# Strassen's seven block products for pairs of FFN input column blocks, with weight sums made by adding DMA transfers

## The chip, the cores and the metric
One core of one Trainium2 chip. The metric is device time in microseconds of one execution of the whole program; several executions are timed and their median is taken. The engines are TensorE (PE, with its weight loads listed apart as PEld), VectorE (DVE), ScalarE (ACT), GpSimd (POOL) and SyncE (SP), which here only issues DMA transfers; 16 DMA engines move the data.

## The reference
A decoder trunk of two layers on 256 tokens of width 1024, in float32. Each layer is FFN, mixer, FFN, each followed by a LayerNorm; the mixer is a recurrent block in layer 0 and dilated attention in layer 1. So there are four FFNs (numbered 0 to 3 below), and they hold most of the arithmetic:
```python
def swiglu(x, w_in, w_out):            # w_in 1024 x 5632, w_out 2816 x 1024
    gate, up = jnp.split(x @ w_in, 2, axis=-1)
    return (jax.nn.silu(gate) * up) @ w_out
...
x = layer_norm(DEEPNORM_ALPHA * x + 0.5 * swiglu(x, ...), g, b)
```

## The kernel before
**Precision.** Weights and activations are split into a high part (rounded to fp32r) and a low part (the rest), and each product of 128x128 by 128xN is three matmuls, hi*hi, hi*lo and lo*hi (`mm3`, L90, all recorded as L88).

**Weights.** All weights come from HBM in halves of 128 x 1024 floats (512 KB). `half_piece` (L117) makes one half ready: SP loads it into a `raw` buffer (L126; 4 of them), ACT casts raw to `w_hi` (L127), DVE subtracts to get `w_lo` (L128). There are 10 buffers of `w_hi` and `w_lo` (`WBUFS`). `order_ffn` and its like write the order of all halves into the list `feed`; `pump` emits the next half, `take` hands out the next piece of two halves and pumps what is missing. A cast needs a free weight buffer, so it waits until PE has done with the half ten places earlier; a load needs a free raw buffer, so SP waits for the subtraction four halves earlier. Outside the blocks marked `pinned` the framework's list scheduler orders each engine's queue; each queue then runs strictly in order.

**An FFN** (`ffn`, L337) runs over 11 column blocks j of 256 gate and 256 up columns. In block j, `natural` (L309) multiplies for both token halves t the x of 128 tokens (transposed and split in `xT`) with the block's two w_in pieces: 8 row blocks times 3 matmuls of 512 columns into one PSUM bank, so 48 matmuls. `gate` (L345) makes silu(gate) * up * 0.5 (ACT L347, DVE L350); its `rest` (L352) turns the result on PE (L98) and splits it into `h_hi` and `h_lo` (L104, L105), put off by `flush` to the next block. Then `prj.part` multiplies h of block j-2 with its w_out piece: 24 matmuls of 512 columns into four more banks (`yy`). The last three w_out pieces form the tail, in `Project.finish` (L279), together with LayerNorm (`Norm`, L229; its power, L245, is POOL's only work after the start) and the turning of the new x into `xT`.

**Order of the work.** FFN 0, the recurrent stage, FFN 1, keys and values, FFN 2, attention, FFN 3. The recurrent stage follows a list of steps written out by hand, `RG` (L463), in which `pv` is one pumped half, letters are steps (u, y, g, o on PE; h, b, q, z, e on ACT; and so on); inside `pinned` the engines keep that order. In FFN 0 the late loads (`late_loads`, L196: x for the LayerNorm, parameters, a distance table) and `softplus_prep` stand inside block 4, behind its `natural` (L415).

Of the kernel before, what the change touches and what calls it, by code (L numbers as in the profile page):

```python
# [9 lines left out]
F32 = mybir.dt.float32  # L10
F32R = mybir.dt.float32r
AF = mybir.ActivationFunctionType
ALU = mybir.AluOpType
# [20 lines left out]
PIECE = 2048  # L34
HALF = PIECE // 2
TAIL = 3
WBUFS = 10
KVBUFS = 12
WARM = 17
PRE = 2  # L40
HBUFS = 6
DILATIONS = ((128, 1), (512, 4), (2048, 16))
SLOPES = [float(2.0 ** (-8.0 * (i + 1.0) / HEADS)) for i in range(HEADS)]
# [3 lines left out]
def trunk_kernel(  # L47
# [36 lines left out]
    def two_banks():  # L84
        return psum.tile([P, 1024], F32, name="yy", bufs=2)

    def mm(ps, lhsT, rhs, start, stop):
        tc.keep_in_program_order(nc.tensor.matmul(ps, lhsT=lhsT, rhs=rhs, start=start, stop=stop))  # L88

    def mm3(ps, a, b, first, last):  # L90

        (ahi, alo), (bhi, blo) = a, b
        mm(ps, ahi, bhi, first, False)
        mm(ps, ahi, blo, False, False)
        mm(ps, alo, bhi, False, last)

    def turn(ps, src):
        tc.keep_in_program_order(nc.tensor.transpose(ps, src, ident))  # L98
# [8 lines left out]
    def duo(tag, bufs, pool=act, shape=(2, SEQ)):  # L107
        hi = pool.tile([P, *shape], F32R, name=f"{tag}_hi", bufs=bufs)
        lo = pool.tile([P, *shape], F32R, name=f"{tag}_lo", bufs=bufs)
        return hi, lo  # L110
# [6 lines left out]
    def half_piece(src, low=nc.vector, cuts=1, high=nc.scalar):  # L117
        if low is None:
            w = wts.tile([P, HALF], F32, name="w_full", tag="w_hi", bufs=WBUFS)
            nc.sync.dma_start(w, src)  # L120
            return w
        raw = wts.tile([P, HALF], F32, name="raw", bufs=4)
        w = duo("w", WBUFS, wts, (HALF,))
        for n in range(cuts):
            c = slice(n * HALF // cuts, (n + 1) * HALF // cuts)
            nc.sync.dma_start(raw[:, c], src[:, c])  # L126
            (nc.scalar.copy if high is nc.scalar else high.tensor_copy)(w[0][:, c], raw[:, c])  # L127
            i = low.tensor_tensor(out=w[1][:, c], in0=raw[:, c], in1=f32(w[0][:, c]), op=ALU.subtract)  # L128
        if low in barrier:
            tc.add_manual_dep(i.ins, barrier[low].ins.name, NO_SYNC, reason="after the LayerNorm")  # L130
        return w
# [7 lines left out]
    def pump(n=1, low=None, high=nc.scalar):  # L139

        for _ in range(min(n, len(feed))):
            src, e, cuts = feed.pop(0)
            ready.append(half_piece(src, e and (low or e), cuts, high))

    def take(n=2):

        pump(n - len(ready))
        w, ready[:n] = ready[:n], []
        return w
# [46 lines left out]
    def late_loads():  # L196
        for dst_, src in ((xn[0], x[tok(0), :]), (xn[1], x[tok(1), :]), (par, rg_par), (dst, dist), (qsc, q_scale)):
            tc.keep_in_program_order(nc.sync.dma_start(dst_, src))
# [20 lines left out]
    def load_ln(i, tag="o", bufs=4):  # L219
        gb = [[act.tile([P, 512], F32, name="gb", tag=f"{tag}_{('hi', 'lo')[j]}", bufs=bufs) for j in range(2)]  # L220
              for _ in range(2)]
        for r in range(2):
            for h in range(2):
                tc.keep_in_program_order(
                    nc.sync.dma_start(gb[r][h], ln[i, r, h * 512:(h + 1) * 512].partition_broadcast(P)))
        return gb
# [91 lines left out]
    def channels(ps, w):  # L318

        for m in range(2):  # L320
            channel_half(ps[:, m * SEQ:(m + 1) * SEQ], w, m)

    def order_ffn(idx):
        if not idx:
            for n in range(8):
                h = n // 2 % 2
                order(w_in[idx, 2 * (n % 2) + n // 4], cuts=1 if n else 2, only=slice(h, h + 1))
        for j in range(NJ):
            for q in range(2):
                if idx or j > 1:  # L330
                    order(w_in[idx, 2 * j + q])
            if 0 <= j - 2 < NJ - TAIL:
                order(w_out[idx, j - 2])
        for i in range(NJ - TAIL, NJ):
            order(w_out[idx, i])

    def ffn(ln_i, turn_x, ahead):  # L337
        hs, gated = {}, {}
        later = []

        def flush(keep=0):
            while len(later) > keep:
                later.pop(0)()

        def gate(ps, t, j):  # L345
            sg = work.tile([P, 256], F32, name="sg")
            nc.scalar.activation(sg, ps[:, :256], AF.Silu)  # L347
            if t == 0:
                gated[j] = work.tile([P, NT, 256], F32, name="gated", tag="sc")
            nc.vector.scalar_tensor_tensor(gated[j][:, t, :], ps[:, 256:], 0.5, sg, ALU.mult, ALU.mult)  # L350

            def rest():  # L352
                hh = gated.pop(j)
                pt = bank()
                for m in range(2):
                    for t_ in range(NT):
                        turn(pt[:, (m * NT + t_) * P:(m * NT + t_ + 1) * P], hh[:, t_, m * P:(m + 1) * P])
                split(*hs[j], halves(pt))
            if t:
                later.append(rest)  # L360

        prj = Project(lambda t, k: at(hs[k // 2], k % 2, tok(t)), KF)
        for j in range(2):
            hs[j] = duo("h", HBUFS)
        if turn_x:
            gb = load_ln(ln_i)
            w = [take() for _ in range(3)]
            opened = []
            for t in range(NT):
                ps = bank()  # L370
                natural(ps, t, w[:2])
                flush()
                gate(ps, t, 0)
                if t == 0:
                    turn_x(0)
                ps = bank()
                natural(ps, t, w[2:], range(4))
                opened.append(ps)
                if t == 0:
                    turn_x(1)  # L380
            w3 = take()
            for t in range(NT):
                natural(opened[t], t, (None, w3), range(4, 8))
                flush()
                gate(opened[t], t, 1)
        else:
            with pinned():
                ps = [[bank() for _ in range(NT)] for _ in range(2)]
                for q in range(4):
                    if q:  # L390
                        load_xT(2 * q, 2 * q + 1)
                    else:
                        load_xT(0)
                    for j in range(2):
                        w = take(1)
                        if q == j == 0:
                            load_xT(1)
                        for t in range(NT):
                            natural(ps[j][t], t, {q // 2: {q % 2: w[0]}}, range(2 * q, 2 * q + 2))
                pump(PRE)  # L400
                for j in range(2):
                    for t in range(NT):
                        gate(ps[j][t], t, j)
                    if j == 0:
                        pump(4 - PRE)
        for j in range(2, NJ):
            hs[j] = duo("h", HBUFS)
            w = [take() for _ in range(2)]
            for t in range(NT):
                ps = bank()  # L410
                natural(ps, t, w)
                flush(1 - t if j == 2 else 0)
                gate(ps, t, j)
            if j == 4 and not turn_x:
                late_loads()  # L415
                gb = load_ln(ln_i)
                softplus_prep()
            if 0 <= j - 2 < NJ - TAIL:
                w = take()
                for t in range(NT):  # L420
                    prj.part(t, j - 2, w)
        for i in range(NJ - 2, NJ - TAIL):
            w = take()
            for t in range(NT):
                prj.part(t, i, w)
        tail = [(i, take()) for i in range(NJ - TAIL, NJ)]
        first, second = prj.tail(tail)
        first[2:5] = first[3], first[2], first[4]
        return prj.finish([first, second], gb, (ahead,), flush)
# [15 lines left out]
    def natural_pair(turn_x, then):  # L445
# [3 lines left out]
        for t, ps in enumerate(natural_both(turn_x)):  # L449
# [3 lines left out]
            def rest(t=t, tmp=tmp):  # L453
# [6 lines left out]

    ENGINES = {"v": (nc.vector, nc.scalar), "g": (nc.gpsimd, nc.scalar),
               "V": (nc.vector, nc.vector), "G": (nc.gpsimd, nc.vector)}
    RG = """r0 pv u3 pv pv pv r1 c1 c0 pv pv u2 pv pv u4 pv pv pv pv pv g0 c4 h0 pv pv g1 c2 h1 y0 g2 pv e0 pv y1  # L463
        c3 h2 pv b0 b2 g3 pv g4 pv h3 pv y3 a2 h4 pv b3 pv b4 b1 q01 y2 q34 a01 a34 e1 z1 e3 m01 e2 z0 s0 m4
        s1 F0 F1 z2 y4 pv e4 m3 k0 z4 o0 s4 q2 k1 m2 s2 F2 z3 s3 o1 k2 F4 o2 pv F3 pv k4 k3 T21101""".split()

    def order_recurrent():
        both = (nc.vector, nc.vector)
# [348 lines left out]
        order(o_w[i])  # L817
    order_ffn(3)

    turn_x = ffn(0, None, 4)  # L820
    with pinned():
        turn_x = recurrent(1, turn_x)
    turn_x = ffn(2, turn_x, 4)
    kv = keys_values(turn_x)
    pump(6)
    turn_x = ffn(3, lambda h: None, 4)
    with pinned():
        turn_x = attention(kv, 4, turn_x)
    ffn(5, turn_x, 0)


# [74 lines left out]
```

## Time and profile before
| | |
|---|---|
| median of 3 runs | 1055.94 us (1055.44 to 1056.11) |
| the profiled execution | 1054.88 us, of which the span from the first to the last instruction is 1052.8 |
| PE, DVE, ACT, POOL busy | 1033.1, 650.5, 524.9, 11.9 us |
| matmuls and their like on PE | 5305 |
| HBM read | 190.75 MB |

The profile is that of one execution. A group of instructions is named by its line, engine and operation and by the tile that it writes and those that it reads; "idle before" is the time for which the engine stood still just ahead of the group, with what ended it. The ends of matmuls are modelled, so PE counts as busy also where matmuls run slower than they could; the distance from one start to the next is the safer reading.

### The profile page before, as it was taken

The numbers are of one execution on the slowest core, as the hardware profiler recorded it, in microseconds if no ns is written. First come the engines' busy times: TensorE is split into PE (matmuls) and PEld (weight loads), VectorE is DVE, ScalarE is ACT, GpSimd is POOL, SyncE is SP. The second block draws the span as 40 slices with busy tenths as digits, with TensorE's granted clock in tenths as the row PEclk, the third lists the DMA queues.
The fourth block names the chain that finished last, engine by engine and source line by source line (L and its number), as shares of the span: only waits on it lengthen the run. The fifth ranks groups of instructions, "written<-read, shape, count | busy, mean of one in ns | idle before, by whom it ended". The sixth has DMA issues, their size and how long they took to land.

```text
span 1052.8 us, 13746 instructions
## 1 busy us (share of the span) xinstructions
PE 1033.1 (98%) x5305; PEld 867.1 (82%) x5305; DVE 650.5 (62%) x847; ACT 524.9 (50%) x730; POOL 11.9 (1%) x18
## 2 busy tenths in 40 slices
PE   9999999999899999999999999999999999999997
PEld 7888888899778888888898888888999678888885
DVE  5764555685987454557745555556787887454544
ACT  6664443369846344443535444342776746343430
POOL 0000000000000000000000000000000000000000
PEclk9999999999999999999999999999999999999999
DMA  8885546184358655542856455651533548555521
GB/s 286 285 297 187 198 162 200 42 299 164 118 194 264 209 178 194 194 167 82 276 202 236 164 200 175 206 177 63 178 124 100 181 152 271 203 173 201 189 92 40
DMA packets 55648, 192.69 MB, mean 183 GB/s; under 512 B 6432, under 2 KB 6688, under 8 KB 55584
## 3 DMA queue, kind: packets, MB, share of 16 engines
q1 hardware_dynamic: 55584, 191.83, 53.8%
q8 instruction: 41, 0.67, 0.2%
q14 instruction: 23, 0.19, 0.1%
HBM read 190.75 MB, written 1.05 MB: 182 GB/s over the span
## 4 chain that ended last, share of the span: by engine, by line
PE 89%; ACT 4%; DVE 4%; DMA 1%; issue 1%; POOL 0%; SPq 0%; DVEq 0%; ACTq 0%; POOLq 0%
PE mm L88 57%; PE yy L88 29%; PE mm L98 3%; DVE w_lo L128 1%; ACT w_hi L127 1%; ACT th L101 1%; ACT L101 1%; DVE xn L237 0%; DMA raw<-in_w_in_dram 0%; DMA raw<-in_o_w_dram 0%; ACT sc L726 0%; DVE xn L250 0%; ACT aa L101 0%; DVE st L238 0%; DVE xT L105 0%
## 5 line engine op out<-in xcount | busy, mean ns | idle before, releaser
L128 DVE TENSOR_TENSOR w_lo<-raw,w_hi 128x1024 fp32r<-128x1024 f32 (+1 forms) x343 | 413.5, 1220 | 216.3 <-ACT w_hi L127 205.6
L88 PE MATMUL mm<-w_hi,xT 128*128 128x512 f32 x1536 | 494.4, 394 | 0.6 <-DVE xT L105 0.6
L127 ACT CAST w_hi<-raw 128x1024 fp32r<-128x1024 f32 (+1 forms) x342 | 353.9, 1049 | 234.6 <-PE yy L88 114.5
L88 PEld LDWEIGHTS mm<-w_hi,xT 128*128 128x128 f32 x1536 | 288.3, 188 | 63.2 <-DVE xT L105 2.6
L88 PE MATMUL mm<-w_lo,xT 128*128 128x512 f32 x768 | 299.9, 390 | 0.7 <-DVE w_lo L128 0.7
L88 PEld LDWEIGHTS mm<-w_lo,xT 128*128 128x128 f32 x768 | 144.5, 188 | 31.0 <-DVE w_lo L128 2.4
L88 PE MATMUL yy<-w_hi,h_hi 128*128 128x512 f32 x352 | 138.3, 393 | 0.0
L88 PE MATMUL yy<-w_hi,h_lo 128*128 128x512 f32 x352 | 137.1, 390 | 0.0
L88 PE MATMUL yy<-w_lo,h_hi 128*128 128x512 f32 x352 | 137.0, 389 | 0.0
L347 ACT ACTIVATE sg<-mm 128x256 f32<-128x256 f32 x88 | 33.8, 384 | 156.3 <-PE mm L88 154.9
L350 DVE SCALAR_TENSOR_TENSOR gated<-mm,sg 128x256 f32<-128x256 f32 x88 | 36.9, 420 | 105.7 <-ACT sg L347 105.5
L88 PE MATMUL mm<-xT,w_hi 128*128 128x256 f32 x480 | 88.6, 286 | 0.0
L88 PEld LDWEIGHTS yy<-w_hi,h_lo 128*128 128x128 f32 x352 | 66.1, 188 | 13.9
L88 PEld LDWEIGHTS yy<-w_lo,h_hi 128*128 128x128 f32 x352 | 66.1, 188 | 13.4
L88 PEld LDWEIGHTS yy<-w_hi,h_hi 128*128 128x128 f32 x352 | 66.1, 188 | 13.2
L88 PEld LDWEIGHTS mm<-xT,w_hi 128*128 128x128 f32 x480 | 74.7, 191 | 2.4 <-issue 2.0
L88 PE MATMUL mm<-xT,w_lo 128*128 128x256 f32 x240 | 67.9, 283 | 0.0
L88 PEld LDWEIGHTS mm<-xT,w_lo 128*128 128x128 f32 x240 | 45.9, 191 | 0.0
L104 ACT CAST xT<-mm 128x512 fp32r<-128x512 f32 x20 | 11.7, 586 | 60.0 <-PE mm L98 59.9
L88 PE MATMUL yy<-xT,w_hi 128*128 128x256 f32 x224 | 41.2, 286 | 0.0
L105 DVE TENSOR_TENSOR h_lo<-mm,h_hi 128x512 fp32r<-128x512 f32 x44 | 30.4, 690 | 13.2 <-ACT h_hi L104 13.2
L88 PEld LDWEIGHTS yy<-xT,w_hi 128*128 128x128 f32 x224 | 35.1, 192 | 0.2
(109 smaller groups left out, 708.2 us busy)
## 6 DMA issues: line engine op xcount, KB each, us to landing
raw<-in_w_in_dram SPq DMA_DIRECT2D x175, 512.0 KB, 4.4
raw<-in_w_out_dram SPq DMA_DIRECT2D x88, 512.0 KB, 5.0
raw<-in_q_w_dram SPq DMA_DIRECT2D x20, 512.0 KB, 4.5
raw<-in_rg_in_dram SPq DMA_DIRECT2D x16, 512.0 KB, 5.1
gb<-in_ln_dram SPq DMA_DIRECT2D x24, 256.0 KB, 5.9
raw<-in_rg_out_dram SPq DMA_DIRECT2D x10, 512.0 KB, 4.0
raw<-in_v_w_dram SPq DMA_DIRECT2D x8, 512.0 KB, 4.9
raw<-in_k_w_dram SPq DMA_DIRECT2D x8, 512.0 KB, 5.6
```

Of the source, the lines that this page charges most:

```text
L88: tc.keep_in_program_order(nc.tensor.matmul(ps, lhsT=lhsT, rhs=rhs, start=start, stop=stop))
L98: tc.keep_in_program_order(nc.tensor.transpose(ps, src, ident))
L101: tc.keep_in_program_order(nc.scalar.activation(dst_, src, f, **kw))
L104: nc.scalar.copy(hi, src)
L105: nc.vector.tensor_tensor(lo, src, f32(hi), ALU.subtract)
L127: (nc.scalar.copy if high is nc.scalar else high.tensor_copy)(w[0][:, c], raw[:, c])
L128: i = low.tensor_tensor(out=w[1][:, c], in0=raw[:, c], in1=f32(w[0][:, c]), op=ALU.subtract)
L347: nc.scalar.activation(sg, ps[:, :256], AF.Silu)
L350: nc.vector.scalar_tensor_tensor(gated[j][:, t, :], ps[:, 256:], 0.5, sg, ALU.mult, ALU.mult)
```

## The change
Two FFNs, numbers 1 and 3, treat two pairs of column blocks, (3, 4) and (7, 8), in another way (`PAIRS`). For a pair, x is cut into four blocks (2 token halves by 2 halves of the inner dimension) and the weights into four (a, b above, c, d below: 2 halves of the inner dimension by 2 column blocks). In place of eight block products there are seven (the Winograd form of Strassen's scheme), each of 4 x 3 matmuls of 512 columns:

- `sum_x`, once per FFN in block 2, makes the four sums and differences of x blocks (s1 to s4) on DVE and splits them; they live in the 12 `kv` tiles.
- `combined` makes the weight operands: a; a+b; d; a+b+d; c; b+d; a+b+c+d. SP loads a, b, c and d as before. A sum is made in the raw buffer: GpSimd issues a DMA transfer from HBM that adds to what the buffer holds (`accum_op=ALU.add`). Each operand's two halves are cast and subtracted as before, from the raw buffer, between one addition and the next. So a pair has 8 plain loads and 8 adding ones in place of 8 plain loads for w_in, and 14 halves to split in place of 8.
- `two_blocks` runs the products in the order a, a+b, (w_out of block j-2), d, a+b+d, c, b+d, (w_out of j-1), a+b+c+d, in three PSUM banks, and puts the four results together with 2 ACT copies and 5 DVE additions or subtractions of 128x512.

Beside that: weight buffers 10 to 9 and raw buffers 4 to 6 for the whole kernel, a new order of the list `RG` with the same steps, and the late loads moved from behind block 4's `natural` to behind its w_out part.
```diff
-WBUFS = 10
+WBUFS = 9
+RAWBUFS = 6
+PAIRS = {1: (3, 7), 3: (3, 7)}
...
+LATE = 5
...
+    def combined(idx, j):
...
+        def load(name, h):
+            q, n = divmod("abcd".index(name), 2)
+            raw[name, h] = wts.tile([P, HALF], F32, name="raw", bufs=RAWBUFS)
+            nc.sync.dma_start(raw[name, h], w_in[idx, 2 * (j + n) + q][:, h * HALF:(h + 1) * HALF])
+
+        def plus(out, name, h):
+
+            q, n = divmod("abcd".index(name), 2)
+            nc.gpsimd.dma_start(raw[out, h], w_in[idx, 2 * (j + n) + q][:, h * HALF:(h + 1) * HALF], accum_op=ALU.add)
+
+        def parts(name, h):
+            w = duo("w", WBUFS, wts, (HALF,))
+            split(w[0], w[1], raw[name, h])
+            return w
...
+        def second(h):
+            load("b", h)
+            plus("b", "a", h)
+            return parts("b", h)
+
+        def third(h):
+            plus("b", "d", h)
+            return parts("b", h)
...
+        def fifth(h):
+            plus("d", "b", h)
+            return parts("d", h)
...
+        def last(h):
+            plus("b", "c", h)
+            return parts("b", h)
+
+        return [lambda f=f, h=h: f(h)
+                for f in (first, second, fourth, third, sixth, fifth, last) for h in range(2)]
...
     def order_ffn(idx):
...
+            if j in PAIRS.get(idx, ()):
+                sums = combined(idx, j)
+                feed.extend(sums[:4])
+                order(w_out[idx, j - 2])
+                feed.extend(sums[4:12])
+                order(w_out[idx, j - 1])
+                feed.extend(sums[12:])
+                continue
...
+        def product(ps, lhs, first=True, last=True):
+            w = take()
+            for k in range(4):
+                mm3(ps, lhs(k), cols(w, k * 512, 512), first and k == 0, last and k == 3, skip_group_check=True)
+
+        def two_blocks(j):
...
+            a, b, c = (bank() for _ in range(3))
+            product(a, part(0, 0), True, False)
+            nc.scalar.copy(flat(0), a)
+            product(c, named("s1"), True, False)
+            nc.scalar.copy(flat(1), c)
+            flush()
+            w = take()
+            for t in range(NT):
+                prj.part(t, j - 2, w)
+            product(c, named("s4"), False)
+            product(b, named("s2"), True, False)
+            nc.vector.tensor_tensor(flat(2), b, flat(0), ALU.add)
+            product(a, part(1, 0), False)
+            nc.vector.tensor_tensor(flat(3), c, flat(2), ALU.subtract)
+            gate(flat(3), 0, j + 1)
+            gate(a, 0, j)
+            product(b, named("s3"), False, False)
+            nc.vector.tensor_tensor(flat(2), b, flat(0), ALU.add)
+            nc.vector.tensor_tensor(flat(1), flat(1), flat(2), ALU.subtract)
+            gate(flat(1), 1, j + 1)
+            w = take()
+            for t in range(NT):
+                prj.part(t, j - 1, w)
+            product(b, part(1, 1), False)
+            nc.vector.tensor_tensor(flat(0), b, flat(0), ALU.add)
+            flush()
+            gate(flat(0), 1, j)
```

## Rows read from the trace of the kernel before
**Rows 1.** The page: span, and busy time, share and instructions of each engine.
```profile
span 1052.8 us, 13746 instructions
...
PE 1033.1 (98%) x5305; PEld 867.1 (82%) x5305; DVE 650.5 (62%) x847; ACT 524.9 (50%) x730; POOL 11.9 (1%) x18
```
**Rows 2.** The page: shares of the chain that ended last, by engine.
```profile
PE 89%; ACT 4%; DVE 4%; DMA 1%; issue 1%; POOL 0%; SPq 0%; DVEq 0%; ACTq 0%; POOLq 0%
```
**Rows 3.** That chain in order of time, FFN 3: start us, us, what.
```profile
868.44 10.92 PE mm L88 x48
...
893.45 0.44 PE mm L98 x4
893.89 5.48 PE yy L88 x24
899.37 5.44 PE mm L88 x24
```
**Rows 4.** Stretches, blocks 2, 3, 4 of FFN 3: busy us of each engine, clock, DMA.
```profile
core 0: us, PE busy (x) PEld busy (x) DVE busy (x) ACT busy (x) POOL busy (x), PEclk, DMA share, GB/s
...
882.60:899.40 16.80, 16.80 (x77) 13.91 (x76) 11.35 (x14) 9.35 (x14) 0.00 (x0) 1.00 0.81 274
899.40:916.20 16.80, 16.80 (x77) 13.90 (x76) 8.71 (x9) 7.45 (x10) 0.00 (x0) 1.00 0.52 181
916.20:933.00 16.80, 16.80 (x77) 13.91 (x77) 8.71 (x9) 7.47 (x10) 0.00 (x0) 1.00 0.53 177
```
**Rows 5.** Timeline of ACT, block 3 of FFN 3: start, us, what, [idle before, releaser].
```profile
906.67 1.05 ACT L127 CAST w_hi<-raw 128x1024 fp32r<-128x1024 f32 x1 [0.81 <-PE mm L88]
908.06 1.06 ACT L127 CAST w_hi<-raw 128x1024 fp32r<-128x1024 f32 x1 [0.33 <-PE mm L88]
909.42 1.06 ACT L127 CAST w_hi<-raw 128x1024 fp32r<-128x1024 f32 x1 [0.30 <-PE mm L88]
```
**Rows 6.** Groups by shape: count, busy us, mean ns, idle before and its releasers.
```profile
L128 DVE TENSOR_TENSOR w_lo<-raw,w_hi 128x1024 fp32r<-128x1024 f32 x341 | 412.2, 1223 | 214.6 <-ACT w_hi L127 203.9
L127 ACT CAST w_hi<-raw 128x1024 fp32r<-128x1024 f32 x340 | 352.7, 1052 | 233.0 <-PE yy L88 114.5 <-PE mm L88 59.6 <-DMA raw<-in_w_in_dram 39.7
...
L350 DVE SCALAR_TENSOR_TENSOR gated<-mm,sg 128x256 f32<-128x256 f32 x88 | 36.9, 420 | 105.7 <-ACT sg L347 105.5
...
L347 ACT ACTIVATE sg<-mm 128x256 f32<-128x256 f32 x88 | 33.8, 384 | 156.3 <-PE mm L88 154.9 <-issue 1.4
...
L105 DVE TENSOR_TENSOR h_lo<-mm,h_hi 128x512 fp32r<-128x512 f32 x44 | 30.4, 690 | 13.2 <-ACT h_hi L104 13.2
...
L104 ACT CAST h_hi<-mm 128x512 fp32r<-128x512 f32 x44 | 25.8, 586 | 10.0 <-PE mm L98 8.3
...
L451 ACT COPY nat<-mm 128x512 f32<-128x512 f32 x4 | 2.4, 589 | 3.9 <-PE mm L88 3.9
```
**Rows 7.** DMA: SP's queue on the page, and the densest stretch (as rows 4).
```profile
q1 hardware_dynamic: 55584, 191.83, 53.8%
...
40.00:60.00 20.00, 20.00 (x93) 16.55 (x92) 13.39 (x31) 12.13 (x17) 0.00 (x0) 1.00 0.95 330
```
**Rows 8.** Waits: who waited for whom, us in total, times, longest.
```profile
POOL rs L245 <- DVE rs L244: 1035.6, 12, 222.6
...
ACT spt L204 <- DMA par<-in_rg_par_dram: 2.3, 1, 2.3
...
SPq L126 <- DVE w_lo L128: 769.4, 284, 22.2
```
**Rows 9.** Timeline of ACT where attention ends (as rows 5).
```profile
854.12 1.05 ACT L127 CAST w_hi<-raw 128x1024 fp32r<-128x1024 f32 x1 [1.77 <-PE yy L88]
855.77 1.05 ACT L127 CAST w_hi<-raw 128x1024 fp32r<-128x1024 f32 x1 [0.60 <-DMA raw<-in_w_in_dram]
856.89 0.59 ACT L104 CAST xT<-mm 128x512 fp32r<-128x512 f32 x1
```
**Rows 10.** Recurrent stage: timeline of PE, and one stretch (as rows 4).
```profile
269.84 0.28 PE L88 MATMUL mm<-xT,w_lo 128*128 128x256 f32 x1
273.23 0.72 PE L88 MATMUL yy<-w_hi,kv 128*128 128x512 f32 x1 [3.12 <-ACT kv L104]
...
272.00:279.00 7.00, 5.46 (x17) 3.93 (x18) 6.42 (x11) 6.05 (x9) 0.00 (x0) 0.76 0.23 75
```

More of the change, by code (lines that the diff above doesn't have):

```diff
@@ L85, in two_banks, with mm, mm3 @@
         return psum.tile([P, 1024], F32, name="yy", bufs=2)
-    def mm(ps, lhsT, rhs, start, stop):
-        tc.keep_in_program_order(nc.tensor.matmul(ps, lhsT=lhsT, rhs=rhs, start=start, stop=stop))
-    def mm3(ps, a, b, first, last):
+    def mm(ps, lhsT, rhs, start, stop, **kw):
+        tc.keep_in_program_order(nc.tensor.matmul(ps, lhsT=lhsT, rhs=rhs, start=start, stop=stop, **kw))
+    def mm3(ps, a, b, first, last, **kw):
         (ahi, alo), (bhi, blo) = a, b
-        mm(ps, ahi, bhi, first, False)
-        mm(ps, ahi, blo, False, False)
-        mm(ps, alo, bhi, False, last)
+        mm(ps, ahi, bhi, first, False, **kw)
+        mm(ps, ahi, blo, False, False, **kw)
+        mm(ps, alo, bhi, False, last, **kw)
     def turn(ps, src):
@@ L121, in half_piece @@
             return w
-        raw = wts.tile([P, HALF], F32, name="raw", bufs=4)
+        raw = wts.tile([P, HALF], F32, name="raw", bufs=RAWBUFS)
         w = duo("w", WBUFS, wts, (HALF,))
@@ L141, in pump @@
         for _ in range(min(n, len(feed))):
-            src, e, cuts = feed.pop(0)
+            item = feed.pop(0)
+            if callable(item):
+                ready.append(item())
+                continue
+            src, e, cuts = item
             ready.append(half_piece(src, e and (low or e), cuts, high))
@@ L321, in channels, with first, fourth, sixth @@
             channel_half(ps[:, m * SEQ:(m + 1) * SEQ], w, m)
+    def combined(idx, j):
+        raw = {}
+        def load(name, h):
[9 more added lines that the diff above has]
+            return w
+        def first(h):
+            load("a", h)
+            return parts("a", h)
+        def second(h):
[5 more added lines that the diff above has]
+            return parts("b", h)
+        def fourth(h):
+            load("d", h)
+            return parts("d", h)
+        def fifth(h):
+            plus("d", "b", h)
+            return parts("d", h)
+        def sixth(h):
+            load("c", h)
+            return parts("c", h)
+        def last(h):
[3 more added lines that the diff above has]
+                for f in (first, second, fourth, third, sixth, fifth, last) for h in range(2)]
     def order_ffn(idx):
@@ L328, in order_ffn @@
         for j in range(NJ):
+            if j - 1 in PAIRS.get(idx, ()):
+                continue
+            if j in PAIRS.get(idx, ()):
[5 more added lines that the diff above has]
+                feed.extend(sums[12:])
+                continue
             for q in range(2):
@@ L335, in order_ffn, with ffn, sum_x, whole @@
             order(w_out[idx, i])
-    def ffn(ln_i, turn_x, ahead):
+    def ffn(ln_i, turn_x, ahead, pairs=()):
         hs, gated = {}, {}
         later = []
+        sums = {}
+        def sum_x():
+            sums["tmp"] = v = [act.tile([P, 4, P], F32, name="v", tag="kv", bufs=KVBUFS) for _ in range(4)]
+            def whole(dst_, q, t):
+                hi, lo = at(xT, slice(4 * q, 4 * q + 4), tok(t))
+                nc.vector.tensor_tensor(dst_, f32(hi), f32(lo), ALU.add)
+            def keep(name, src):
+                pair = [act.tile([P, 4, P], F32R, name="s", tag="kv", bufs=KVBUFS) for _ in range(2)]
+                split(pair[0], pair[1], src)
+                sums[name] = pair
+            whole(v[0], 0, 0)
+            whole(v[1], 0, 1)
+            nc.vector.tensor_tensor(v[2], v[0], v[1], ALU.subtract)
+            keep("s3", v[2])
+            whole(v[3], 1, 1)
+            nc.vector.tensor_tensor(v[1], v[1], v[3], ALU.subtract)
+            keep("s1", v[1])
+            nc.vector.tensor_tensor(v[0], v[1], v[0], ALU.subtract)
+            keep("s2", v[0])
+            whole(v[3], 1, 0)
+            nc.vector.tensor_tensor(v[3], v[3], v[0], ALU.add)
+            keep("s4", v[3])
+        def product(ps, lhs, first=True, last=True):
[3 more added lines that the diff above has]
+        def two_blocks(j):
+            xs = [act_.rearrange("p k s -> p (k s)") for act_ in sums["tmp"]]
+            flat = lambda n: xs[n]
+            part = lambda q, t: (lambda k: at(xT, 4 * q + k, tok(t)))
+            named = lambda n: (lambda k: at(sums[n], k))
+            a, b, c = (bank() for _ in range(3))
[25 more added lines that the diff above has]
+            gate(flat(0), 1, j)
@@ L406, in ffn @@
         for j in range(2, NJ):
+            if j == LATE and not turn_x:
+                late_loads()
+                gb = load_ln(ln_i)
+                softplus_prep()
+            if j - 1 in pairs:
+                continue
             hs[j] = duo("h", HBUFS)
+            if j in pairs:
+                hs[j + 1] = duo("h", HBUFS)
+                two_blocks(j)
+                continue
             w = [take() for _ in range(2)]
@@ L413, in ffn @@
                 gate(ps, t, j)
[L414 to L417, printed above, removed]
+            if j == 2 and pairs:
+                sum_x()
             if 0 <= j - 2 < NJ - TAIL:
@@ L462, in trunk_kernel @@
                "V": (nc.vector, nc.vector), "G": (nc.gpsimd, nc.vector)}
-    RG = """r0 pv u3 pv pv pv r1 c1 c0 pv pv u2 pv pv u4 pv pv pv pv pv g0 c4 h0 pv pv g1 c2 h1 y0 g2 pv e0 pv y1
-        c3 h2 pv b0 b2 g3 pv g4 pv h3 pv y3 a2 h4 pv b3 pv b4 b1 q01 y2 q34 a01 a34 e1 z1 e3 m01 e2 z0 s0 m4
-        s1 F0 F1 z2 y4 pv e4 m3 k0 z4 o0 s4 q2 k1 m2 s2 F2 z3 s3 o1 k2 F4 o2 pv F3 pv k4 k3 T21101""".split()
+    RG = """pv u3 pv pv pv r0 pv pv r1 c1 pv u2 pv u4 pv c0 g0 pv c2 pv pv c4 pv g1 pv pv h0 h1 pv y0 pv c3 e0 pv
+        g2 h2 b2 y1 pv b0 g3 pv h3 pv pv g4 h4 y2 pv a2 b4 b1 b3 a01 y3 q01 a34 e2 q34 y4 z0 m01 e1 z1 s0 s1
+        m4 F1 F0 z2 pv e4 k0 k1 z4 e3 q2 s4 m3 o0 m2 z3 s2 F4 F2 o1 s3 k2 o2 pv F3 pv k4 k3 T21101""".split()
     def order_recurrent():
@@ L818, in trunk_kernel @@
     order_ffn(3)
-    turn_x = ffn(0, None, 4)
+    turn_x = ffn(0, None, 4, PAIRS.get(0, ()))
     with pinned():
         turn_x = recurrent(1, turn_x)
-    turn_x = ffn(2, turn_x, 4)
+    turn_x = ffn(2, turn_x, 4, PAIRS.get(1, ()))
     kv = keys_values(turn_x)
@@ L828, in trunk_kernel @@
         turn_x = attention(kv, 4, turn_x)
-    ffn(5, turn_x, 0)
+    ffn(5, turn_x, 0, PAIRS.get(3, ()))
 def kernel(**inputs):
```

## The prediction, made before the changed kernel ran
> **What bounds the kernel now.** I read the page's busy times first, then the chain of waits, then the chain in order of time, and last the stretches of one feed-forward network (FFN). PE is busy 98% of the span, and the chain that ended last lies 89% on it [rows 1, 2]; the reader should see that the next engine, DVE, has 62%. Inside an FFN the chain is PE and nothing else: 48 matmuls of 512 columns take 10.92 us, or 0.2275 us each, four transposes take 0.44, and the 24 matmuls of a w_out piece 5.48 [rows 3]. A block is therefore 10.9 + 0.4 + 5.5 = 16.8 us, and in a block in steady state DVE works 8.7 us, ACT 7.5, and the DMA engines are busy for 52% [rows 4]. PE's work is the price; whatever the other engines gain or lose counts only when they fall behind.
>
> **Ahead of PE** the weights stand ready: the casts of ACT in a steady block wait for a PE matmul, not for a DMA [rows 5], because the ten weight buffers are full and PE must give one back. So PE has some ten halves in hand.
>
> **The change, part by part.**
>
> *Seven products for eight.* Two blocks take 96 matmuls of 512 columns on w_in; seven products of 12 take 84. The shapes stay (stationary 128x128, moving 512), so the price of one stays: 12 x 0.2275 = 2.73 us per pair, and with two pairs in each of two FFNs 48 matmuls, **-10.9 us**. Transposes and w_out matmuls are as many as before. This is the one term on the critical path for certain.
>
> *Work on DVE and ACT in a pair.* A pair of blocks lasts 33.6 us now and would last 30.9. DVE subtracts 18 halves (14 sums or blocks, 4 of w_out) at 1.22 us = 22.0, makes 5 additions of 512 columns (nearest row: h_lo, also one PSUM and one SBUF input, 0.69) = 3.5, four gates at 0.42 = 1.7, two h_lo = 1.4: 28.5 of 30.9 us. ACT casts 18 halves at 1.05, copies 2 banks at 0.59, has 4 Silu at 0.38 and 2 h_hi at 0.59: 22.8 us [rows 6]. Both fit, DVE barely. What hides it is the lead of nine halves, and the two plain blocks between the pairs, in which DVE idles 2 x 8.1 us [rows 4]. Gone that cover, each microsecond that DVE overruns would be one of PE. The sums of x (sum_x) add 12 operations of 512 columns on DVE, 12 x 0.69 = 8.3 us, and 4 casts on ACT, once per FFN in block 2, where DVE had 16.8 - 11.4 = 5.4 us idle [rows 4]; 3 us of them run into the lead. Cost 0.
>
> *Banks.* The sixth product adds on to the bank that DVE must have read after the fourth; the fifth product, 2.73 us, lies between. An addition behind one subtraction already begun needs 1.22 + 0.69 = 1.9 us: in time. Behind two it needs 3.1, so 0.4 us late. I take from 0 to 4 x 0.4 = 1.6 us, and 0.5.
>
> *Adding DMA transfers.* No row of this trace shows one, nor any DMA issued by GpSimd. A plain half of 512 KB is worth this much time of the 16 DMA engines: 53.8% of 1052.8 us for 191.83 MB [rows 7], so 0.524 MB cost 1.55 us; at the densest stretch, 330 GB/s at 95% [rows 7], it is 1.51. A pair now needs 12 plain halves, 18.6 us; after the change 12 plain and 8 adding. Let an add cost x. It moves the same bytes from HBM, so x is not under 1.55; as it also has to read what it adds to, I put it at two reads, 3.1 us, and leave 6.2 as the far end. What must be served when: counting from the pair's start, PE finishes the products at 2.7, 5.5, (w_out to 10.9), 13.7, 16.4, 19.1, 21.9, (w_out to 27.3), 30.1. With nine buffers the cast of item n waits for the release of item n-9; so the second product's sums are split at about -17 to -7, and the later adds (two each of d, b, c) start behind that; the last must land at 25, one split ahead of its product. In those 41 us go 6 adds and 8 plain halves, 12.4 us: the DMA engines keep up to x = (41 - 12.4) / 6 = 4.8 us. At 1.55 or at 3.1 the sum has no term: 0. Each microsecond of x above 4.8 costs 4 pairs x 6 = 24 us.
>
> The Trainium skill, "Collectives: The Full Stack", section "The bandwidth ceiling: the fold count and why AG ≠ RS ≠ AR", says that an add in the DMA engines reads two sources through one ring and so moves half the bytes of a copy in the same time; no run here shows it. By that an add costs two copies, and the sum above stays as it is with the lead, but not without it (the first rival).
>
> *GpSimd's queue* gets 8 issues per pair, each waiting for the split that still reads its buffer, with the next add behind it. The only other work on it is LayerNorm's power, 12 times in the span [rows 8], never inside a pair. Cost 0, with 5 us or more between an add's start and its need.
>
> *Nine weight buffers, six raw.* A cast waits for one half's release more. In the middle of an FFN this is lead only. Where a stage ends, ACT's queue is in order, and a cast that waits for PE holds back the xT cast behind it, as the 1.77 us wait at 854 us does [rows 9]. Bounds: 0, and one half, 2.7 us, at each of five stage ends. I take 1.0 in all, nearer to 0, because only casts issued in a stage's last few microseconds stand ahead of xT. Two more raw buffers let loads start earlier, which is worth 0 while casts wait for PE.
>
> *The list RG* moves the recurrent stage's steps; the matmuls are the same. The stage has one real hole: PE ends a matmul at 270 and starts the next at 273.23, 3.3 us after it could, and then the granted clock is 0.76 over 7 us [rows 10]: 7 x 0.24 / 0.5 = 3.4 us at 1.2 GHz after PE had stood idle, worth 1.7. A new order can close this (-5) or double it (+5). I can't tell which, so 0. *LATE* lets two w_out halves, 3.1 us of DMA, go ahead of the late loads. All but par are read at the end of that FFN; for par ACT waits 2.3 us now [rows 8], with the casts behind it, and some 3 us more stay within the lead. Cost 0.
>
> **Sum:** -10.9 + 0.5 + 1.0 = -9.4 us. Against the profiled execution, 1054.88 us (span 1052.8 and 2.1 around it), that is 1045.5; the median of the runs stands 1.06 above that execution, so 1046.5.
>
> **Rivals.**
> *The DMA engines become the bound (slower).* For it: in a pair 12 x 1.55 + 8 x 3.1 = 43.4 us of transfers stand against 30.9 us of PE. If buffers kept by the sums of b (two of six raw from the second product to the last) stop the loads from running ahead, all 12.5 us per pair are waited for: +50, some 1095 us. With the lead it decides from x = 4.8 us, and passes the time of before at 5.2; at x = 6.2 it is +34, some 1080. Against it: SyncE now waits for buffers, not for bandwidth (769 us behind w_lo [rows 8]). This is where the skill's rule on adds would bring the slower result. Chance 0.18, all of it slower.
> *The gain is given back outside the pairs.* The hole in the recurrent stage doubles (+5), casts at the stage ends come late by a half in two or three places (+5): 1051 to 1060. For it: every stage before was ordered for ten buffers; against it: RG was redone. Chance 0.17, of which 0.08 are still faster, 0.06 the same, 0.03 slower.
> *The hole closes as well.* -10.9 - 3.3 and, if the clock stays up, -1.7: 1040.5 to 1043. Chance 0.08.
>
> **How the numbers follow.** The forecast, 1043 to 1051, has 0.57. About 0.2%, 2.1 us, is what a measurement of this kernel can tell from no change. Faster: 0.57 + 0.08 + 0.08 = 0.73; the same 0.06; slower 0.18 + 0.03 = 0.21. The range runs from 1040.5, where the hole is closed, to 1060, the end of the second rival, and leaves out the first rival alone, 0.18.
>
> **What would show it.** Right: in groups mm<-w_hi and mm<-w_lo on PE together 48 matmuls of 512 columns fewer; between the first matmul of a pair and the first of the block behind it 30.9 us; ACT's casts in pairs still waiting for PE. Wrong: PE waiting on w_hi or w_lo in a pair, and ACT's casts waiting for DMA raw (first rival, with the adds' time from issue to landing and the DMA share near 1); PE gaps over 3 us with a lower clock in the recurrent stage, or xT casts late behind a weight cast (second rival); PE waiting for a DVE addition ahead of the sixth product (my bank term).

## The result, and the profile after

The changed kernel takes 1067.21 us (median of 4 runs, 1066.56 to 1068.4) against 1056.03 of the kernel before on the same chip: a ratio of 1.0107, interval [1.0093, 1.012]. The forecast was 1046.5 with a range of 1040.5 to 1060, so it was wrong in sign. The profiled execution took 1066.56 us. One execution of a version below (two pairs, six additions on GpSimd) ran at a granted clock of 0.752, took 1275.22 us and is left out of that version's numbers.

The page of the changed kernel: busy times, two DMA queues (packets, MB, share of the 16 engines), the chain that ended last, DMA issues (count, KB each, median us to landing):

```profile
span 1064.8 us, 13925 instructions
...
PE 1028.7 (97%) x5257; PEld 861.7 (81%) x5257; DVE 699.8 (66%) x915; ACT 554.9 (52%) x770; POOL 40.0 (4%) x50
...
q1 hardware_dynamic: 55584, 191.83, 52.2%
q0 software_dynamic: 4608, 16.78, 8.6%
...
PE 76%; DMA 9%; DVE 8%; ACT 4%; issue 3%; POOL 0%; SPq 0%; DVEq 0%; ACTq 0%; POOLq 0%
...
raw<-in_w_in_dram SPq DMA_DIRECT2D x175, 512.0 KB, 5.2
raw<-in_w_out_dram SPq DMA_DIRECT2D x88, 512.0 KB, 5.4
raw<-in_w_in_dram POOLq DMA_DIRECT2D x32, 512.0 KB, 7.8
```

The 48 matmuls are gone (5305 in [rows 1], 5257 here), yet the chain, which lay 89% on PE [rows 2], lies on it for 76% only: DMA and DVE hold 17% of it, where they held 5%. All 32 additions of GpSimd's queue q0 together took 8.6% of 1064.8 us, so 2.86 us of the 16 engines each; a plain half took 52.2% of 1064.8 us for 191.83 MB, so 1.52 us per 0.524 MB. An adding transfer costs 1.88 plain ones. (The Trainium skill, "Collectives: The Full Stack", section "The bandwidth ceiling: the fold count and why AG ≠ RS ≠ AR", says of the adds of a collective that they need two source reads and so run at half the rate of a copy; for the adding transfers here the trace agrees within 6%.)

Who waited for whom (us in total, times, longest), PE of the changed kernel:

```profile
PE mm L91 <- DVE v L460: 14.3, 4, 5.0
PE yy L91 <- ACT kv L107: 4.7, 1, 4.7
```

L460 is the addition that must empty bank b before the sixth product writes it: four pairs, four waits. In PE's timeline the matmul after each hole starts 3.65, 3.61, 5.15 and 2.56 us later than 0.23 us behind the one before, 15.0 us in all. From the first matmul of a pair to the first of the block behind it the four pairs take 36.10, 34.52, 38.33 and 35.01 us (the first from 347.87 to 383.97), where the prediction had 30.9. The hole of the first pair, read back along the chain (start us, us, what):

```profile
355.17 10.47 DMA raw<-in_w_out_dram
...
365.74 1.06 ACT w_hi L130
...
366.82 0.04 DVE w_lo L131
...
369.10 1.22 DVE w_lo L108
370.32 0.61 DVE v L460
```

and DVE's timeline over the same stretch (start, us, what, [idle before, releaser]):

```profile
363.40 1.22 DVE L131 TENSOR_TENSOR w_lo<-raw,w_hi 128x1024 fp32r<-128x1024 f32 x1 [1.59 <-ACT w_hi L130]
366.82 1.23 DVE L131 TENSOR_TENSOR w_lo<-raw,w_hi 128x1024 fp32r<-128x1024 f32 x1 [2.19 <-ACT w_hi L130]
367.96 2.35 DVE L108 TENSOR_TENSOR w_lo<-raw,w_hi 128x1024 fp32r<-128x1024 f32 x2
370.24 0.68 DVE L460 TENSOR_TENSOR v<-mm,v 128x512 f32<-128x512 f32 x1
```

The fourth product's last matmul starts at 364.46, so the addition could start near 364.7 (the run with the gate first, below, starts it at 364.52); it starts at 370.24. Ahead of it in DVE's queue stand four subtractions of weights that nobody needs yet: two of the w_out piece of block j-1 (L131) and two of the pair's last operand (L108). The first two wait for ACT's casts, and these for w_out halves that took up to 10.47 us to land, where 5.0 was the median before. Why they landed late is in the stretches (us, busy of PE, PEld, DVE, ACT, POOL, clock, DMA share, GB/s; the share counts a packet's whole time where it starts, so it can pass 1):

```profile
352.00:356.00 4.00, 4.00 (x21) 3.32 (x20) 3.32 (x4) 2.99 (x5) 0.88 (x2) 1.00 1.05 205
...
360.00:364.00 4.00, 4.00 (x19) 3.30 (x18) 1.82 (x2) 1.61 (x2) 0.00 (x0) 1.00 1.05 274
...
370.00:374.00 4.00, 2.94 (x7) 2.39 (x8) 4.00 (x6) 2.21 (x4) 0.00 (x0) 0.62 0.90 283
374.00:378.00 4.00, 4.00 (x18) 3.26 (x18) 3.94 (x7) 2.10 (x2) 0.00 (x0) 0.95 0.88 329
...
434.00:446.00 12.00, 8.54 (x38) 6.73 (x38) 10.34 (x13) 8.46 (x10) 0.00 (x0) 1.00 0.82 270
924.00:940.00 16.00, 11.01 (x39) 8.63 (x38) 12.66 (x15) 9.58 (x12) 0.00 (x0) 0.79 0.85 292
996.00:1006.00 10.00, 7.60 (x27) 5.86 (x26) 9.92 (x13) 6.13 (x9) 0.00 (x0) 0.83 0.84 277
```

From 352 to 364 the DMA engines are full while they deliver 205 to 274 GB/s; the kernel before got 330 out of a share of 0.95 [rows 7]. Six additions were issued from 341.27 to 352.57, because GpSimd waited for the subtractions that still read its buffers (the wait view of POOL has 45.3 us in 21 waits behind w_lo L108), and the w_out loads were issued behind them, from 353.73 on. The lines from 370 on, two behind the first hole and one around each of the other three, show what a hole costs besides itself: around the restart of PE the granted clock falls below 1.00, which means part of the stretch at 1.2 GHz. Three of the four holes have such a stretch, with 3.4, 6.8 and 3.4 us at the lower level. The second of them began at 927.36, while PE stood still until 929.31, so 11.6 of these 13.6 us lie behind a restart, and 11.6 / 2 = 5.8 us were lost. With the holes that is 20.8 us; the four pairs together took 20.9 us more than 4 x 30.77, the time of a pair without a hole in the next run.

### The profile page after: what moved, and what is told of

Read it like the earlier page. It is cut to its first block, busy times and chain, and to the rows that moved or that the text cites. A ratio compares the mean times of both kernels' runs of the same rounds, so it can differ in the third digit from the quotient of the medians.

```text
span 1064.8 us, 13925 instructions
## 1 busy us (share of the span) xinstructions
PE 1028.7 (97%) x5257; PEld 861.7 (81%) x5257; DVE 699.8 (66%) x915; ACT 554.9 (52%) x770; POOL 40.0 (4%) x50
## 3 DMA queue, kind: packets, MB, share of 16 engines
q1 hardware_dynamic: 55584, 191.83, 52.2%
HBM read 207.53 MB, written 1.05 MB: 196 GB/s over the span
## 4 chain that ended last, share of the span: by engine, by line
PE 76%; DMA 9%; DVE 8%; ACT 4%; issue 3%; POOL 0%; SPq 0%; DVEq 0%; ACTq 0%; POOLq 0%
PE mm L91 47%; PE yy L91 27%; DMA raw<-in_w_in_dram 5%; DMA raw<-in_w_out_dram 4%; DVE w_lo L131 3%; PE mm L101 2%; DVE w_lo L108 1%; ACT w_hi L130 1%; ACT w_hi L107 1%; DVE xT L108 1%; DVE xn L257 1%; DVE xn L244 1%; DVE st L245 1%; ACT th L104 0%; ACT L104 0%
## 5 line engine op out<-in xcount | busy, mean ns | idle before, releaser
L131 DVE TENSOR_TENSOR w_lo<-raw,w_hi 128x1024 fp32r<-128x1024 f32 (+1 forms) x311 | 373.7, 1218 | 160.4 <-ACT w_hi L130 152.3
L91 PE MATMUL mm<-w_hi,xT 128*128 128x512 f32 x1376 | 443.8, 394 | 0.6 <-DVE xT L108 0.6
L130 ACT CAST w_hi<-raw 128x1024 fp32r<-128x1024 f32 (+1 forms) x310 | 318.3, 1048 | 201.4 <-PE yy L91 103.4
L91 PEld LDWEIGHTS mm<-w_hi,xT 128*128 128x128 f32 x1376 | 257.9, 188 | 57.1 <-DVE xT L108 2.8
L91 PE MATMUL mm<-w_lo,xT 128*128 128x512 f32 x688 | 268.5, 390 | 1.2 <-DVE w_lo L131 1.2
L91 PEld LDWEIGHTS mm<-w_lo,xT 128*128 128x128 f32 x688 | 129.3, 188 | 28.5 <-DVE w_lo L131 3.0
L108 DVE TENSOR_TENSOR w_lo<-raw,w_hi 128x1024 fp32r<-128x1024 f32 x56 | 67.2, 1222 | 33.5 <-ACT w_hi L107 33.1
L107 ACT CAST w_hi<-raw 128x1024 fp32r<-128x1024 f32 x56 | 57.7, 1050 | 48.4 <-PE yy L91 25.9
L91 PE MATMUL mm<-w_hi,s 128*128 128x512 f32 x128 | 45.7, 425 | 14.3 <-DVE v L460 14.3
L91 PEld LDWEIGHTS mm<-w_hi,s 128*128 128x128 f32 x128 | 26.7, 209 | 21.8 <-ACT w_hi L130 15.9
```

The costliest lines, as they stand in the source:

```text
L107: nc.scalar.copy(hi, src)
L108: nc.vector.tensor_tensor(lo, src, f32(hi), ALU.subtract)
```

## The experiments

Two theories stood against each other: the order of DVE's queue (ready work behind work that is not) and the price of the additions in the DMA engines.

**The additions' price taken away, every queue kept.**

```diff
-            nc.gpsimd.dma_start(raw[out, h], w_in[...], accum_op=ALU.add)
+            nc.gpsimd.dma_start(raw[out, h], w_in[...])
```

> The changed kernel with the 32 adding transfers of GpSimd replaced by plain ones of the same bytes to the same buffers (the additions are left out); all engines' queues keep their order. The page of the changed kernel gives an add 8.6% of 16 engines' span over 32 transfers, 2.86 us, against 1.52 us of a plain half. Theory that the second read of an add makes the landings late: 8 x 1.34 = 10.7 us less per pair on the DMA engines, the w_out halves land in time although the addition still stands behind them, the holes fall under 1 us each, about 1045 to 1048 us. Rival (the fixed time of GpSimd's issues and the chain of buffers make them late, not the engines' time): holes of 2.5 to 5 us stay, 1060 us or more.

Measured: 1046.42 us (1045.71 to 1047.56), ratio 0.9904 [0.9891, 0.9918]. From the page, and the same stretch as above:

```profile
q0 software_dynamic: 4608, 16.78, 4.7%
```

```profile
352.00:356.00 4.00, 4.00 (x21) 3.33 (x20) 3.56 (x5) 3.79 (x6) 1.07 (x2) 1.00 0.79 243
```

The same transfers of the same bytes from the same queue now cost 4.7% of 1045.8 us over 32, 1.54 us each, and the share falls from 1.05 to 0.79. No hole over 0.3 us is left in any pair, and a pair takes 30.8 to 31.1 us, with the same order of instructions on every engine. The doubling belongs to the adding. Without it the order does next to no harm, but the margin is thin: L460 still stands behind the same four subtractions.

**DVE's order changed, the additions kept.** The subtractions of w_out j-1 and of the last operand are told, by a dependency without a semaphore, to stand behind L460.

```diff
+            early = nc.vector.tensor_tensor(flat(2), b, flat(0), ALU.add)
...
+            barrier[nc.vector, "sum"] = early; w = take()
...
+            after_sum(split(w[0], w[1], raw[name, h]))
```

> The changed kernel, with one edit of order: on DVE the first addition of a pair (the read of bank b behind the fourth product) goes ahead of the subtractions for the w_out piece of j-1 and for the last operand; no transfer, matmul or wait for data is changed. Queue theory (the sixth product waits because DVE's queue has the addition behind subtractions whose transfers land late): the four holes ahead of the sixth products, 3.65 + 3.61 + 5.15 + 2.56 = 15.0 us, and about 6.8 us lost to the lower clock behind them go, so 1067.2 - 21.8 = about 1045 us. Rival (the DMA engines are the bound in the pair, and the queue only shows it): the late halves are then waited for by PE itself, the holes move to the w_out piece or the seventh product, and the time stays over 1058 us.

Measured: 1061.8 us (1059.28 to 1063.25), ratio 1.0047 [1.0031, 1.0062]. That is over the rival's 1058, but not by the rival's cause: PE waits for w_lo for 0.8 us in all, and it did so for 0.7 in the kernel before. The waits at L460 are gone; PE has four new ones (its waits, then ACT's timeline ahead of the first):

```profile
PE mm L101 <- DVE gated L486: 9.7, 4, 3.7
```

```profile
381.45 1.06 ACT L130 CAST w_hi<-raw 128x1024 fp32r<-128x1024 f32 x1 [1.56 <-DMA raw<-in_w_out_dram]
385.13 1.04 ACT L130 CAST w_hi<-raw 128x1024 fp32r<-128x1024 f32 x1 [2.62 <-DMA raw<-in_w_in_dram]
386.38 1.04 ACT L130 CAST w_hi<-raw 128x1024 fp32r<-128x1024 f32 x1 [0.20 <-DMA raw<-in_w_in_dram]
387.33 0.58 ACT L107 CAST h_hi<-mm 128x512 fp32r<-128x512 f32 x1
387.80 0.42 ACT L483 ACTIVATE sg<-v 128x256 f32<-128x256 f32 x1
```

The same fault, one step later and on another engine: the Silu of the pair's last gate stands in ACT's queue behind casts that wait for late halves, and PE waits for that gate to turn h. One edit of order moved the wait and took 5.4 us off; neither theory had this.

**The last gate first as well.** The casts and subtractions of w_out and of the next block also stand behind the pair's last gate, on ACT and DVE.

```diff
+            sums["gate"] = silu, nc.vector.scalar_tensor_tensor(...)
...
+            w = [take() for _ in range(2)]; j - 2 in pairs and barrier.update({(e, "gate"): i for e, i in zip((nc.scalar, nc.vector), sums["gate"])})
```

> The kernel of e1_sum_first with a second edit of order: in the block behind a pair, ACT's casts and DVE's subtractions for w_out and for the block after it come behind the pair's last gate (the trace of e1 has its four holes, 3.9 + 2.4 + 2.9 + 1.4 = 10.5 us, where PE waits to turn that gate, held up by casts that wait for DMA). Queue theory (PE never lacks weights; only work that is ready stands behind work whose data lands late): the four holes and the lower clock behind them, 5 us, go: 1061.8 - 15 = about 1046 to 1048 us, as fast as with plain transfers. DMA theory (the engines' time is short by itself): PE now waits for w_hi or w_lo in or behind the pairs, in sum 8 us or more, 1055 us or more.

Measured: 1047.9 us (1047.24 to 1048.47), ratio 0.9922 [0.9905, 0.9938], with the additions as dear as ever. The page, two stretches and a line of DVE's timeline:

```profile
q0 software_dynamic: 4608, 16.78, 8.6%
...
PE 78%; DVE 7%; DMA 7%; ACT 4%; issue 2%; POOL 1%; SPq 0%; DVEq 0%; ACTq 0%; POOLq 0%
```

```profile
352.00:356.00 4.00, 4.00 (x21) 3.27 (x21) 3.13 (x3) 3.23 (x6) 0.87 (x1) 1.00 1.05 189
...
368.00:372.00 4.00, 4.00 (x19) 3.33 (x18) 1.12 (x3) 4.00 (x7) 0.00 (x0) 1.00 0.61 230
```

```profile
364.52 0.69 DVE L460 TENSOR_TENSOR v<-mm,v 128x512 f32<-128x512 f32 x1 [3.50 <-PE mm L91]
```

The DMA engines are as full as in the changed kernel, and the time is within 1.5 us of plain transfers. L460 now waits for PE, as it should. Three of the four pairs take 30.8 to 31.0 us; the last takes 32.4, with waits of PE of 0.21 us for the w_lo of a w_out half and of 0.64 us for the addition L466, so late landings still cost a little there. So a late landing and a queue that puts ready work behind it were both needed; taking away the first, or the second on both engines, brings the forecast time. The shares of the chain by themselves would not have told: here it lies on PE for 78% and on DMA for 7%, hardly otherwise than in the changed kernel, which is 19.3 us slower.

**Nine and six buffers, the new RG and LATE, without pairs.**

```diff
-PAIRS = {1: (3, 7), 3: (3, 7)}
+PAIRS = {}
```

> The changed kernel without any pair: nine weight buffers, six raw ones, the new RG list and the moved late loads alone. My theory from the LayerNorm times of the two traces: the recurrent stage is 2.1 us longer (its hole 4.9 us in place of 3.4, its lower clock 6.8 us in place of 3.4), the rest within 0.5 us, so before + 2 us, about 1058. Rival of the prediction (the stage ends come late by a half each): before + 4 us or more. If the buffers and the order had paid: before or less.

Measured: 1056.78 us (1055.69 to 1058.92), ratio 1.0006 [0.9997, 1.0015]. Without pairs these parts cost nothing that can be told from zero, less than the 2 us expected; the harm lies in the pairs.

**Six of the eight additions on an engine.** On top of the gate first, the additions of a, d and c into b are made between raw buffers, first on DVE, then on GpSimd; the two of b into d stay transfers.

```diff
+            nc.gpsimd.dma_start(...) if out == "d" else nc.vector.tensor_tensor(out=raw[out, h], in0=raw[out, h], in1=raw[name, h], op=ALU.add)
```

> As e5, but six of the eight additions of a pair (a to b, d to a+b, c to a+b+d) are made by DVE in the raw buffers from blocks that are loaded anyway; only b to d stays an adding transfer. Per pair 6 x 2.86 = 17 us less on the DMA engines and 6 x 1.22 = 7.3 us more on DVE: 35.8 us of 30.9, to be lent by the plain blocks, which have 8 us each. If e5 is held by the DMA engines: as fast as plain transfers or a little faster, 1044 to 1048. If DVE becomes the bound, PE waits for w_lo in the pairs, up to 5 us each: 1050 to 1066.

> As e6 with the six additions on GpSimd, whose time for 128 x 1024 float32 with two inputs no run here has shown; bounds: DVE's 1.22 us and four times that, so 7 to 29 us per pair on an engine that does nothing else there. If it runs beside DVE: as e6 at best or better, 1044 to 1048. If DVE's subtractions get longer than 1.22 us while GpSimd adds, that shows in their mean in the pairs, and the time is over 1050.

Measured: 1046.01 us (1045.78 to 1046.23), ratio 0.9902 [0.9887, 0.9917], on DVE; 1046.52 (1046.27 to 1046.85), ratio 0.9907 [0.9891, 0.9924], on GpSimd. Groups by shape (count, busy us, mean ns), DVE's first and then those with GpSimd:

```profile
L344 DVE TENSOR_TENSOR raw<-raw 128x1024 f32<-128x1024 f32 x24 | 29.2, 1224 | 2.1 <-DMA raw<-in_w_in_dram 2.0
```

```profile
L344 POOL TENSOR_TENSOR raw<-raw 128x1024 f32<-128x1024 f32 x24 | 70.8, 2960 | 128.1 <-DMA raw<-in_w_in_dram 71.1 <-ACT w_hi L107 35.1 <-DVE w_lo L108 21.9
...
L108 DVE TENSOR_TENSOR w_lo<-raw,w_hi 128x1024 fp32r<-128x1024 f32 x56 | 95.6, 1732 | 6.3 <-ACT w_hi L107 6.2
```

and one addition with the subtraction that began during it (start, us, what):

```profile
403.59 2.41 POOL L344 TENSOR_TENSOR raw<-raw 128x1024 f32<-128x1024 f32 x1 [1.16 <-DVE w_lo L108]
...
404.61 2.48 DVE L108 TENSOR_TENSOR w_lo<-raw,w_hi 128x1024 fp32r<-128x1024 f32 x1 [0.16 <-ACT w_hi L107]
```

DVE does 28.5 + 6 x 1.22 = 35.8 us of work for a pair of 30.9 and still PE has no hole in the pairs: the plain blocks before and after cover it. This version is the fastest measured here: all its runs lie under those of the gate first, by 1.9 us in the medians, and its last pair takes 30.8 us where that one took 32.4. GpSimd makes DVE's subtractions beside it slower (a mean of 1732 ns for 1222). The expectation took that for a sign of more than 1050 us; at two pairs per FFN the lead hides it too.

**A third pair, (5, 6), in both FFNs**, so that nothing plain stands between pairs; 24 matmuls fewer again.

```diff
-PAIRS = {1: (3, 7), 3: (3, 7)}
+PAIRS = {1: (3, 5, 7), 3: (3, 5, 7)}
```

> The additions of raw halves on DVE as in e6_sums_on_dve, and a third pair, blocks (5, 6), in FFN 1 and in FFN 3, so that three pairs follow each other. 24 matmuls of 512 columns fewer: -5.5 us of PE, from 1046.0. Theory (what counts is what stands ahead of the work that PE waits for; an engine's total counts once its lead is used up): DVE has 28.5 us of its own work in a pair and 6 additions at 1.22, so 35.8 of the 30.9 us that PE takes. With plain blocks between the pairs (DVE idle 8 us in each) that fitted; with three pairs in a row DVE falls behind by 4.9 us per pair, 14.7 us in one FFN, against a lead of nine halves, some 10 us of PE. So PE should wait on w_lo or on a sum in the third pair, some 5 us per FFN, and the gain of 5.5 us be lost: 1044 to 1052, with PE's waits behind DVE. Rival (the lead and the plain block ahead cover it): 1040.5 and no hole in the pairs.

> The same three pairs with the six additions of raw halves on GpSimd, as in e7_sums_on_gpsimd. DVE's own 28.5 us, plus what the two engines cost each other: 8 additions' worth of slow subtractions (1.73 against 1.22 us, in e7 for those of the sums, 14 per pair) = 7.1 us, so 35.6 of 30.9 us, as much as with the additions on DVE. Theory: the same time as with the additions on DVE, 1044 to 1052, PE's waits behind DVE's w_lo. Rival (DVE's slower subtractions lie beside GpSimd's additions only, and the lead covers them): 1040.5 to 1042.

Measured: 1058.2 us (1057.55 to 1060.4), ratio 1.0021 [1.0009, 1.0034], on DVE; 1091.14 (1089.09 to 1093.88), ratio 1.0332 [1.0301, 1.0362], on GpSimd. With the additions on DVE, PE's waits, one stretch, and DVE's timeline ahead of the holes in FFN 1's second and third pair:

```profile
PE mm L91 <- DVE v L460: 7.8, 4, 3.0
PE yy L91 <- ACT h_hi L107: 4.7, 4, 1.6
```

```profile
430.00:440.00 10.00, 7.03 (x32) 5.55 (x31) 5.88 (x6) 3.14 (x3) 0.00 (x0) 1.00 0.62 168
```

```profile
399.03 1.23 DVE L108 TENSOR_TENSOR w_lo<-raw,w_hi 128x1024 fp32r<-128x1024 f32 x1 [1.46 <-ACT w_hi L107]
400.17 2.35 DVE L344 TENSOR_TENSOR raw<-raw 128x1024 f32<-128x1024 f32 x2
402.44 0.68 DVE L460 TENSOR_TENSOR v<-mm,v 128x512 f32<-128x512 f32 x1
...
436.45 1.23 DVE L108 TENSOR_TENSOR w_lo<-raw,w_hi 128x1024 fp32r<-128x1024 f32 x1 [2.77 <-ACT w_hi L107]
437.59 1.22 DVE L344 TENSOR_TENSOR raw<-raw 128x1024 f32<-128x1024 f32 x1
438.73 0.68 DVE L460 TENSOR_TENSOR v<-mm,v 128x512 f32<-128x512 f32 x1
```

From 340 to 440, from just ahead of FFN 1's first pair until well into its third, DVE is busy for 87.6 us of 100; at L460 PE loses nothing in the first pair, 1.8 us in the second and 3.1 in the third. The direction was as the theory said, the size was not: against two pairs 12.2 us were lost instead of 5.5 won, 8.8 per FFN where some 5 were expected. Nor is DVE simply busy: ahead of the third pair's hole it idles 2.77 us for a cast, and the chain leads from that cast to an adding transfer, issued late behind DVE's own work, that took 8.28 us to land. And the old fault is back: the dependency holds the subtractions behind L460 but not the new additions (L344), and at each of PE's four waits there one or two of them, 1.1 us each, stand ahead of it. In the second pair they are the whole hole, since the w_lo that the sixth product needs too is ready at 400.26, before the fifth product ends. No run orders these additions behind L460, so how much three pairs lose to DVE's amount of work alone stays open. On GpSimd, PE's waits, one of DVE's groups, and DVE's timeline in the first hole:

```profile
PE mm L101 <- DVE gated L486: 14.5, 5, 4.2
PE yy L91 <- ACT h_hi L107: 13.8, 4, 3.7
```

```profile
L108 DVE TENSOR_TENSOR w_lo<-raw,w_hi 128x1024 fp32r<-128x1024 f32 x84 | 136.2, 1657 | 1.1 <-ACT w_hi L107 0.9
```

```profile
387.06 2.93 DVE L131 TENSOR_TENSOR w_lo<-raw,w_hi 128x1024 fp32r<-128x1024 f32 x1
...
390.51 1.97 DVE L486 SCALAR_TENSOR_TENSOR gated<-v,sg 128x256 f32<-128x256 f32 x1
```

That both engines would give the same time fell: 33 us lie between them. The theory priced DVE's slower subtractions as a sum and left out where they stand: in this hole one of them, slowed to 2.93 us, is ahead of the gate that PE waits for, and the gate itself, which reads two SBUF operands as well, is held up too (three records of 1.96, 1.97 and 2.64 us, 0.42 in the mean of [rows 6]). It left out the clock as well: inside the two FFNs five stretches, 37.6 us in all, are at 1.2 GHz, 15.1 of them with PE idle, so 11.2 of the 33 us; with the additions on DVE there is none.

## Why the prediction was wrong, step by step

- **Seven products for eight: right.** Where no hole is left, a pair takes 30.8 us, as forecast. Between the LayerNorm powers on either side, FFN 1 took 485.94 - 309.15 = 176.8 us before and 483.68 - 312.07 = 171.6 with plain transfers, 5.2 less where 24 x 0.2275 = 5.5 was forecast.
- **Work on DVE and ACT: right as a sum** (even 35.8 us of work per 30.9 fitted with two pairs), but only a sum: it says nothing of which instruction stands ahead of which.
- **Banks: this step failed.** It took "an addition behind one subtraction already begun", 0.5 us in all and 1.6 at most. The scheduler had put four subtractions ahead of it, two of them not yet able to start. The term measured 15.0 us of holes and 5.8 at the lower clock. The step bounded the wait by the length of what stands ahead; the bound has to hold what that work itself waits for.
- **Adding transfers: the size right (2.86 us, taken 3.1), the test wrong.** "The DMA engines keep up to x = 4.8 us" spread 6 additions and 8 halves over 41 us. They were issued from 341 to 353, and w_out j-1, issued behind them, was needed on ACT and DVE by 365: some 24 us. Six additions and four halves ask 6 x 2.86 + 4 x 1.52 = 23.2 us of them, the engines were full from 344 on, and a load took 10.47 us. What counted was the landing of single halves, not the mean load.
- **GpSimd's queue: cost 0 for the sums, with too thin a cover.** It asked for 5 us between an addition's start and its need; the landing alone took 7.8 in the median. Still PE waits for the operand of no sum in any version with two pairs. What the queue did do is bunch the additions: five of the six later ones waited for a subtraction just ahead of them.
- **Nine buffers, RG, LATE: right.** 1.0 us was taken; the run without pairs shows 0.7 (1056.78 against 1056.05), interval -0.3 to 1.6. The recurrent hole did not close: PE waits 4.7 us for kv where it waited 3.12 [rows 10], and that stage is 2.1 us longer in the changed profile.
- **The rivals.** The slower one had the right sign and the wrong mechanism: with the gate first the transfers are the same and PE waits for late weights for 0.21 us in all pairs, so the DMA engines were not the bound. The wait that decided stood in the sum at 0.5 us and in the last line of what would show the forecast wrong, but in no rival.

With the terms as the two profiles show them, -10.9 + 15.0 + 5.8 + 2.1 = 12.0 us; the spans differ by 1064.8 - 1052.8 = 12.0.

## What to carry to other kernels

Where a list scheduler writes queues that run strictly in order, read for every short operation that PE waits for what stands ahead of it in its queue and what that work waits for: a late load behind which ready work stands costs its whole lateness. Order such operations ahead of prefetch work by dependencies, on each engine that the chain passes (here DVE and then ACT), before removing load from any engine. An engine may be asked for more than its share in a stretch while a quieter stretch follows soon: two pairs with plain blocks between them fitted. Three in a row did not, but part of that loss is order again, and the share of each is not shown.

## What the runs showed of the hardware that was not expected

- GpSimd and DVE hold each other up when both read two SBUF operands: with GpSimd's additions in two pairs, 41 of the 56 subtractions of 128x1024 took 1207 to 1225 ns and 15 took 2311 to 3434. Each of the 15 began while an addition ran and ended 1.08 to 1.09 us after that addition, as in the two lines shown above (403.59 + 2.41 = 406.00, and 404.61 + 2.48 = 407.09). (The Trainium skill, "SBUF — State Buffer", section "SBUF: two separate sides", calls the port they share an exclusive lock for the whole instruction; the trace agrees with that rather than with an even slowing.)
- Of the changed kernel's four PE holes of 2.6 to 5.2 us three had the lower granted clock at their end or behind it, for 3.4 or 6.8 us; around the one from 437.00 to 440.84 the clock stayed at 1.00. The length of the hole does not decide it alone: with DVE's order changed one of 2.2 us had it, with three pairs on DVE one of 3.1 us had not.
